# A chunked delta rule beside projection matmuls: row stores and half of T's loads on GpSimd's DMA queue, later loads of kq and of late decays, and the third group's masks behind the second substitution

## The chip, the cores and the metric

The kernel runs on one core of a Trainium2 chip. The metric is the device time of one execution in microseconds (us); less is better. The engines have short names in the profile: PE is TensorE (matmuls), DVE is VectorE, ACT is ScalarE, POOL is GpSimd, SP is SyncE, which here only issues DMAs. GpSimd issues DMAs too, on a queue of its own.

## The reference

One layer of a hybrid backbone: a SwiGLU FFN, then two mixers side by side (a 2-D neighbourhood attention and a bidirectional gated delta rule), merged by gates, then a second FFN; 512 latent and 256 context tokens of width 1024. The change lies in the delta rule, which the reference computes by chunks:

```python
def gated_delta_chunks(q, k, v, g, beta, s0, with_output):
    ...
    decay = jnp.exp(jnp.where(lower, g[..., :, None] - g[..., None, :], -jnp.inf))
    k_beta = k * beta[..., None]
    m = jnp.where(strict, jnp.einsum('...ik,...jk->...ij', k_beta, k) * decay, 0.0)
    rhs = jnp.concatenate([v * beta[..., None], k_beta * jnp.exp(g)[..., None]], axis=-1)
    uw = lax.linalg.triangular_solve(jnp.eye(GDN_CHUNK, dtype=m.dtype) + m, rhs,
                                     left_side=True, lower=True, unit_diagonal=True)
    ...
    def step(s, xc):
        v_new = xc[0] - jnp.einsum('...ck,...kv->...cv', xc[1], s)
        s_next = s * xc[3][..., None, None] + jnp.einsum('...ck,...cv->...kv', xc[2], v_new)
        ...
        return s_next, (jnp.einsum('...ck,...kv->...cv', xc[4], s)
                        + jnp.einsum('...cj,...jv->...cv', xc[5], v_new))
```

So for each chunk there is a gram matrix of the keys, weighted by decays and beta, a unit lower triangular matrix that has to be inverted, and a scan over the chunks that carries the state S.

## The kernel before, in words

The kernel uses chunks of 128 tokens: six steps s = 0 to 5 (two of context, four of latent tokens), two directions, and four heads in two pairs p = 0, 1. One instruction mostly works on the four matrices of a step and a pair. The steps are treated in three groups of two, called bi = 0, 1, 2 (first, second and third group). Each group passes through these stages:

- `gram` (from line 1114), four times in a group. A decay tile (`Dt`; for some steps a part of an `oacc` tile) is loaded from DRAM (`gcd`, line 1118), VectorE subtracts and masks it (line 1122), ScalarE takes the exponential, and VectorE multiplies it with the products of keys into `Bt` (line 1128), and with those of queries and keys into `At` (line 1134). The products come from TensorE for the steps 0 to 3 (`pq`), and the later steps read the stored ones back (`kq<-kqd`, lines 1096 to 1098), since the two directions meet the same pairs of chunks. `Bt` is stored to DRAM (`bd`).
- `base_inverse` (from line 1140), once in a group. It loads the 32-wide diagonal blocks of all the group's matrices out of `bd` (into `L` and `Ltr`, line 1152), sets L's diagonal to -1 (line 1155), and inverts them all at once by forward substitution on VectorE: 31 rows, each a product (line 1159) and a reduction (line 1160) whose length grows with the row. This is called the substitution here; there are three. The result `Xt` is stored to DRAM (`rd`, line 1163).
- `inverse` (from line 1173), twice in a group. It loads the inverted blocks back as T0 and T1 (`T<-rd`, line 1180, four loads), transposes them on VectorE (lines 1182, 1183), and puts the 128-wide inverse `Tt` together: TensorE `pi` products of 32 and then 64 columns, with copies `Y` and `T` by VectorE and ScalarE between them (lines 1202, 1218, 1229, 1237).
- `scan_step` (from line 1249), four times in a group. TensorE's `pc` products with the state, `r` (line 1260), the values `vn` (line 1269), the new state `S` (line 1284), and from step 2 on the output (`otmp` line 1291, `oacc` lines 1297, 1298).

Between these small steps TensorE does work that waits for nothing in the delta rule: matmuls of the input projection, called fills here (`pm` with `wh`, `wl`, lines 192 to 194; the weight half `wl` comes from VectorE, line 139). `turn` hands out so many fills after each small step.

A scheduler decides the order of the instructions on each engine from the order of the program, the sizes of the tile pools and a model of durations; `tc.issue_after(x)` puts an instruction behind x on its engine. Each engine then runs its own list strictly in order, and so do the DMA queues' issuers: a DMA that waits holds up all that stand behind it on SP. Tile pools matter for the change: `Dt` has two buffers, `kq` two, `r` two.

Of the kernel before, what the change touches and what calls it, by code (L numbers as in the profile page):

```python
# [13 lines left out]
ALU = mybir.AluOpType  # L14
AX = mybir.AxisListType.X
# [3 lines left out]
P = 128  # L19
# [39 lines left out]
def body(ctx, tc, I, out, dbg=None):  # L59
# [1020 lines left out]
    def products(p, s):  # L1080

        def one(n, a, o):
            if s == 1:
                return [kk01[p][:, m ^ 2] for m in range(4)]
            if s < 4:
                t = tl(pgq, [P, 4, P], "pq", 2)
                for m, (d, c, i) in enumerate(mats_of(s)):
                    mm(t[:, m, :], kT[2 * p + i][:, c], a[2 * p + i][:, c - o], start=True, stop=True)
                if s == 0:
                    kk01[p] = t  # L1090
                else:
                    u = tl(gb_, [P, 4, P], "kq", NKQ)
                    S.copy(u[:], t[:])
                    nc.sync.dma_start(kqd[n, s - 2, p], u[:].rearrange("p m c -> p (m c)"))
            else:
                t = tl(gb_, [P, 4, P], "kq", NKQ)
                for h in range(2):
                    nc.sync.dma_start(t[:, 2 * h:2 * h + 2].rearrange("p m c -> p (m c)"), kqd[n, 5 - s, p, :, 256 * (1 - h):256 * (2 - h)])
            return t
        yield one(0, kT, 0)  # L1100
        for _ in range(1 if s > 1 else 4 * s * p):
            turn("g", s // 2)
        if s >= 2:
            yield one(1, qT, 2)
            turn("g", s // 2)

    def decay_place(s, p):

        if s == 2 or s < 2 and p == 1:
            a = 2 * (s == 2)  # L1110
            return oaccs[p if s == 2 else s][:, a:a + 2].rearrange("p a b c -> p (a b) c")
        return tl(gb_, [P, 4, P], "Dt", 2)[:]

    def gram(p, s, bd, g):

        mats = mats_of(s)
        Dt = decay_place(s, p)
        nc.sync.dma_start(Dt[:], bass.AP(gcd.tensor, gcd.offset + (4 * s + 2 * p) * P, [[0, P], [24 * P, 2], [1, 2 * P]]))
        for m, (d, c, i) in enumerate(mats):
            msk = cst[:, (C_MF if d == 0 else C_MB):][:, 0:P]  # L1120
            with tc.issue_after(marks["At" if s > 3 else "Bt"]) if s > 1 else nullcontext():
                V.scalar_tensor_tensor(Dt[:, m], Dt[:, m], gcum[:, d, s, 2 * p + i:2 * p + i + 1], msk, op0=ALU.subtract, op1=ALU.add)
        S.activation(Dt[:], Dt[:], AF.Exp)
        Bt, At = tl(gq, [P, 4, P], "Bt", NBT), None
        for n, t in enumerate(products(p, s)):
            if n == 0:
                for m, (d, c, i) in enumerate(mats):
                    b = V.scalar_tensor_tensor(Bt[:, m], t[m] if s == 1 else t[:, m], beta[:, d, s, 2 * p + i:2 * p + i + 1], Dt[:, m], op0=ALU.mult, op1=ALU.mult)
                if s < 2:
                    marks["Bt"] = b.ins  # L1130
                nc.sync.dma_start(bass.AP(bd.tensor, bd.offset + g * MSTR, [[P, P], [4 * MSTR, 4], [1, P]]), Bt[:])
            else:
                At = tl(gq, [P, 4, P], "At", NAT)
                a = V.tensor_tensor(At[:], t[:], Dt[:], ALU.mult)
                if s < 4:
                    marks["At"] = a.ins
# [3 lines left out]
    def base_inverse(bd, rd):  # L1140
# [8 lines left out]
        st = 32 * P + 32  # L1149
        for q in range(4):  # L1150
            dst = tr[32 * q:32 * q + 32] if q < 2 else L[32 * q:32 * q + 32]
            nc.sync.dma_start(dst, bass.AP(bd.tensor, bd.offset + (q // 2) * 8 * MSTR, [[st, 32], [P, 32], [1, 32]]))
        S.copy(L[0:64].rearrange("p r c -> p c r"), tr[:])

        G.memset(L[:].rearrange("p r c -> p (r c)")[:, 0:1024:33], -1.0)
        for i in range(1, 32):
            c = (i + 1) // 2
            t = tl(gb_, [P, 16, 32], "bt")
            V.tensor_tensor(t[:, 0:c, 0:i + 1], L[:, i:i + 1, 0:i + 1].to_broadcast([P, c, i + 1]), Xt[:, 0:c, 0:i + 1], ALU.mult)
            V.tensor_reduce(Xt[:, 0:c, i], t[:, 0:c, 0:i + 1], AX, ALU.add, negate=True)  # L1160
            if i % 4 == 0:
                yield
        nc.sync.dma_start(bass.AP(rd.tensor, rd.offset, [[512, P], [1, 512]]), Xt[:].rearrange("p c k -> p (c k)"))
        yield


    T6s = [tl(gq, [P, 8, 64], f"T6{i}") for i in range(NT6)]
    Tts = [tl(gq, [P, 8, P], f"Tt{i}") for i in range(NTT)]
    for t in T6s + Tts:
# [3 lines left out]
    def inverse(bi, st, rd, Bts):  # L1173


        T0 = tl(gq, [P, 8, 32], "T0", 2)
        T1 = tl(gq, [P, 8, 32], "T1", 2)
        for dst, d in ((T1, 0), (T0, 1)):
            for q in range(2):
                nc.sync.dma_start(dst[q:P:2, 4 * d:4 * d + 4], bass.AP(rd.tensor, rd.offset + (2 * d + q) * 16384 + st * 2048, [[32, 64], [2 * 2048, 4], [1, 32]]))  # L1180
        fl = lambda t, m: t[:, m:m + 4].rearrange("p m c -> p (m c)")
        V.transpose(fl(T0, 0), fl(T1, 0))
        V.transpose(fl(T1, 4), fl(T0, 4))
        blk = [slice(32 * b, 32 * b + 32) for b in range(4)]

# [732 lines left out]
```

## Time and profile before

| | |
|---|---|
| median of 3 runs | 1499.26 us (1498.73 to 1499.43) |
| the profiled execution's own time | 1495.44 us |
| its span | 1493.7 us |
| TensorE's granted clock, mean | 0.993 |
| TensorE busy | 1434.0 us, 96% |
| VectorE busy | 1144.7 us, 77% |
| ScalarE busy | 661.9 us, 44% |
| GpSimd busy | 212.4 us, 14% |
| the delta rule's groups in the span | about 730 to 966 us |

How to read the rows. A row of the timeline gives the start and the length in us, the engine, the line, the operation with `out<-in`, the shape, the count, and in brackets the idle time before it and what ended it. A row of the waits gives engine, tile and line, what it waited for, then the us in total, the times and the longest. A row of the grouped view gives the count, the busy us, the mean ns of one, and the idle time before with its releaser. A row of the DMA issues gives the queue, the count, the KB of one and the median us from issue to landing.

### The profile page before, as it was taken

The numbers are of one execution on the slowest core, as the hardware profiler recorded it, in microseconds if no ns is written. First come the engines' busy times: TensorE is split into PE (matmuls) and PEld (weight loads), VectorE is DVE, ScalarE is ACT, GpSimd is POOL, SyncE is SP. The second block draws the span as 40 slices with busy tenths as digits, with TensorE's granted clock in tenths as the row PEclk, the third lists the DMA queues.
The fourth block names the chain that finished last, engine by engine and source line by source line (L and its number), as shares of the span: only waits on it lengthen the run. The fifth ranks groups of instructions, "written<-read, shape, count | busy, mean of one in ns | idle before, by whom it ended". The sixth has DMA issues, their size and how long they took to land.

```text
span 1493.7 us, 23926 instructions
## 1 busy us (share of the span) xinstructions
PE 1434.0 (96%) x9117; PEld 1258.3 (84%) x9117; DVE 1144.7 (77%) x1975; ACT 661.9 (44%) x1090; POOL 212.4 (14%) x262
## 2 busy tenths in 40 slices
PE   6999999999999999999998899999999999999997
PEld 4778989999998777888886778877778999998886
DVE  8787869999987565768787886666668799886627
ACT  5433524434333286545544434376526454444310
POOL 1000000000000121223301002243321022220001
PEclk9999999999999999999999999999999999999999
DMA  9676665454559554222577524274344143234732
GB/s 372 211 257 225 222 238 187 137 174 166 170 198 404 181 178 129 84 92 88 159 222 203 167 68 125 92 276 131 100 169 149 64 129 113 85 114 134 263 98 84
DMA packets 109236, 248.56 MB, mean 166 GB/s; under 512 B 29049, under 2 KB 44481, under 8 KB 109121
## 3 DMA queue, kind: packets, MB, share of 16 engines
q1 hardware_dynamic: 104480, 229.40, 46.6%
q0 software_dynamic: 3056, 12.33, 2.2%
q10 hardware_dynamic: 1586, 5.32, 0.9%
q8 instruction: 71, 1.16, 0.3%
q14 instruction: 43, 0.35, 0.1%
HBM read 215.50 MB, written 31.50 MB: 165 GB/s over the span
## 4 chain that ended last, share of the span: by engine, by line
PE 71%; DMA 10%; DVE 9%; ACT 4%; issue 3%; POOL 1%; SPq 1%; DVEq 0%; ACTq 0%; POOLq 0%
PE ps L211 15%; PE pm L192 5%; PE pm L193 5%; PE pm L194 5%; PE ps L533 4%; PE ps L535 4%; PE ps L534 4%; PE ps L1692 3%; PE ps L1694 3%; PE ps L1693 3%; PE ps L193 3%; PE ps L192 3%; PE ps L194 3%; PE pc L1049 3%; DMA wr<-in_up_dram 2%
## 5 line engine op out<-in xcount | busy, mean ns | idle before, releaser
L139 DVE TENSOR_TENSOR wl<-wr,wh 128x1024 fp32r<-128x1024 f32 (+1 forms) x184 | 226.0, 1233 | 112.9 <-ACT wh L137 111.3
L137 ACT CAST wh<-wr 128x1024 fp32r<-128x1024 f32 (+1 forms) x184 | 185.6, 1013 | 278.5 <-PE pm L193 72.7
L192 PE MATMUL pm<-uxh,wh 128*128 128x512 f32 x320 | 131.6, 411 | 0.0
L194 PE MATMUL pm<-uxh,wl 128*128 128x512 f32 x320 | 126.3, 395 | 0.8 <-DVE wl L139 0.8
L193 PE MATMUL pm<-uxl,wh 128*128 128x512 f32 x320 | 126.5, 395 | 0.0
L211 PE MATMUL ps<-wh,hx 128*128 128x512 f32 x352 | 96.1, 391 | 0.1
L211 PEld LDWEIGHTS ps<-wh,hx 128*128 128x128 f32 x352 | 65.9, 188 | 14.5 <-ACT wh L137 0.5
L280 DVE SCALAR_TENSOR_TENSOR adap<-wr,crow 128x1024 f32<-128x1024 f32 x61 | 74.3, 1218 | 2.4 <-DMA wr<-in_w_adaT_dram 1.7
L192 PE MATMUL ps<-uh,wh 128*128 128x256 f32 (+1 forms) x208 | 69.2, 334 | 3.8 <-ACT wh L137 3.8
L194 PEld LDWEIGHTS pm<-uxh,wl 128*128 128x128 f32 x320 | 60.6, 190 | 13.8 <-DVE wl L139 0.9
L192 PEld LDWEIGHTS pm<-uxh,wh 128*128 128x128 f32 x320 | 60.8, 190 | 11.1 <-ACT spill L796 0.2
L193 PEld LDWEIGHTS pm<-uxl,wh 128*128 128x128 f32 x320 | 60.9, 190 | 10.3
L114 POOL TENSOR_TENSOR rs<-ve,mhalf 128x1 f32<-128x1 f32 (+2 forms) x46 | 49.0, 1066 | 140.6 <-DVE ve L110 138.2
L193 PE MATMUL ps<-ul,wh 128*128 128x256 f32 (+1 forms) x208 | 67.9, 327 | 0.0
L194 PE MATMUL ps<-uh,wl 128*128 128x256 f32 (+1 forms) x208 | 67.0, 328 | 0.0
L193 PE MATMUL ps<-uxl,wh 128*128 128x256 f32 (+1 forms) x192 | 60.5, 318 | 2.2 <-DVE uxl L139 2.2
L192 PE MATMUL ps<-uxh,wh 128*128 128x256 f32 (+1 forms) x192 | 59.8, 318 | 1.6 <-ACT uxh L137 1.4
L194 PE MATMUL ps<-uxh,wl 128*128 128x256 f32 (+1 forms) x192 | 60.1, 316 | 0.0
L137 ACT CAST wh<-ra 128x1024 fp32r<-128x1024 f32 x31 | 32.6, 1052 | 59.7 <-PE ps L534 20.2
L533 PE MATMUL ps<-ur,wh 128*128 128x384 f32 x168 | 56.5, 336 | 0.0
L534 PE MATMUL ps<-ur,wh 128*128 128x384 f32 x168 | 56.4, 336 | 0.0
L533 PE MATMUL ps<-uh,wh 128*128 128x384 f32 x168 | 56.4, 336 | 0.0
(502 smaller groups left out, 4252.0 us busy)
## 6 DMA issues: line engine op xcount, KB each, us to landing
wr<-in_w_adaT_dram SPq DMA_DIRECT2D x64, 512.0 KB, 4.7
wr<-in_up_dram SPq DMA_DIRECT2D x56, 512.0 KB, 3.6
wr<-in_win_dram SPq DMA_DIRECT2D x52, 512.0 KB, 3.6
wr<-in_dn_dram SPq DMA_DIRECT2D x51, 512.0 KB, 4.1
ra<-in_up_dram SPq DMA_DIRECT2D x24, 512.0 KB, 4.3
rb<-in_up_dram SPq DMA_DIRECT2D x18, 512.0 KB, 4.0
ra<-in_w_adaT_dram SPq DMA_DIRECT2D x16, 512.0 KB, 5.0
wr<-in_w_o_dram SPq DMA_DIRECT2D x8, 512.0 KB, 4.4
```

What stands on the lines that cost most here:

```text
L114: G.tensor_tensor(rs[:], ve[:], mhalf[:, 0:n], ALU.pow)
L137: S.copy(hi, src)
L139: marks["lo"] = V.tensor_tensor(lo, src, hi.bitcast(F32), ALU.subtract).ins
L192: T.matmul(ps, a, uh[:, k, :], start=(k == 0), stop=False)
L193: T.matmul(ps, a, ul[:, k, :], start=False, stop=False)
L194: marks["mm"] = T.matmul(ps, b, uh[:, k, :], start=False, stop=(k == nk - 1)).ins
L211: T.matmul(banks[t][d][:, c0:c1], a[:, sl], b[:, d * 512 + c0:d * 512 + c1], start=first and j == 0, stop=last and j == 2)
L280: V.scalar_tensor_tensor(pr[:], raw[:], 1.0, crow, op0=ALU.mult, op1=ALU.mult, accum_out=col[:, c:c + 1])
L533: T.matmul(ps[:], a, mh, start=k == 0, stop=False)
L534: T.matmul(ps[:], a, ml, start=False, stop=False)
L535: T.matmul(ps[:], b, mh, start=False, stop=k == 3)
L1049: last[0] = T.matmul(*a, **k).ins
```

## The change

It has five parts.

1. Loads of the stored products for late steps (`kq<-kqd`) and of the decays of the steps 4 and 5 are issued behind the last load of `L` on SP.
2. The decay tile of step 3 is taken from the two `r` buffers instead of the two `Dt` buffers.
3. The masks of the third group are issued behind the last row of the second substitution (before: behind the last `At` of the second group). The stores of step 5's `Bt` are issued behind the last load of T on SP.
4. The store of the rows, `rd`, is issued by GpSimd, and T's loads are issued directly after it, those of T1 by SP and those of T0 by GpSimd. VectorE's first transpose of a pair is issued behind the last `Bt` of step 4's second pair.
5. L's diagonal is set by VectorE instead of GpSimd.

```diff
             else:
                 t = tl(gb_, [P, 4, P], "kq", NKQ)
                 for h in range(2):
-                    nc.sync.dma_start(t[:, 2 * h:2 * h + 2].rearrange("p m c -> p (m c)"), kqd[n, 5 - s, p, :, 256 * (1 - h):256 * (2 - h)])
+                    with tc.issue_after(marks["L"]):
+                        nc.sync.dma_start(t[:, 2 * h:2 * h + 2].rearrange("p m c -> p (m c)"), kqd[n, 5 - s, p, :, 256 * (1 - h):256 * (2 - h)])
...
+        if s == 3:
+            return tl(gq, [P, 4, P], "r", 2)[:]
         return tl(gb_, [P, 4, P], "Dt", 2)[:]
...
-        nc.sync.dma_start(Dt[:], bass.AP(gcd.tensor, gcd.offset + (4 * s + 2 * p) * P, [[0, P], [24 * P, 2], [1, 2 * P]]))
+        with tc.issue_after(marks["L"]) if s > 3 else nullcontext():
+            nc.sync.dma_start(Dt[:], bass.AP(gcd.tensor, gcd.offset + (4 * s + 2 * p) * P, [[0, P], [24 * P, 2], [1, 2 * P]]))
...
-            with tc.issue_after(marks["At" if s > 3 else "Bt"]) if s > 1 else nullcontext():
+            with tc.issue_after(marks["row" if s > 3 else "Bt"]) if s > 1 else nullcontext():
...
-                if s < 2:
+                if s < 2 or (s, p) == (4, 1):
                     marks["Bt"] = b.ins
-                nc.sync.dma_start(bass.AP(bd.tensor, bd.offset + g * MSTR, [[P, P], [4 * MSTR, 4], [1, P]]), Bt[:])
+                with tc.issue_after(marks["Tl"]) if s == 5 else nullcontext():
+                    nc.sync.dma_start(bass.AP(bd.tensor, bd.offset + g * MSTR, [[P, P], [4 * MSTR, 4], [1, P]]), Bt[:])
...
-        G.memset(L[:].rearrange("p r c -> p (r c)")[:, 0:1024:33], -1.0)
+        V.memset(L[:].rearrange("p r c -> p (r c)")[:, 0:1024:33], -1.0)
...
-        nc.sync.dma_start(bass.AP(rd.tensor, rd.offset, [[512, P], [1, 512]]), Xt[:].rearrange("p c k -> p (c k)"))
+        nc.gpsimd.dma_start(bass.AP(rd.tensor, rd.offset, [[512, P], [1, 512]]), Xt[:].rearrange("p c k -> p (c k)"))
+        for st in range(2):
+            T0 = tl(gq, [P, 8, 32], "T0", 2)
+            T1 = tl(gq, [P, 8, 32], "T1", 2)
+            for dst, d in ((T1, 0), (T0, 1)):
+                for q in range(2):
+                    t = (nc.gpsimd if d else nc.sync).dma_start(dst[q:P:2, 4 * d:4 * d + 4], bass.AP(rd.tensor, rd.offset + (2 * d + q) * 16384 + st * 2048, [[32, 64], [2 * 2048, 4], [1, 32]]))
+                    if not d:
+                        marks["Tl"] = t.ins
+            turned.append((T0, T1))
         yield
...
-        T0 = tl(gq, [P, 8, 32], "T0", 2)
-        T1 = tl(gq, [P, 8, 32], "T1", 2)
-        for dst, d in ((T1, 0), (T0, 1)):
-            for q in range(2):
-                nc.sync.dma_start(dst[q:P:2, 4 * d:4 * d + 4], bass.AP(rd.tensor, rd.offset + (2 * d + q) * 16384 + st * 2048, [[32, 64], [2 * 2048, 4], [1, 32]]))
+        T0, T1 = turned.pop(0)
         fl = lambda t, m: t[:, m:m + 4].rearrange("p m c -> p (m c)")
-        V.transpose(fl(T0, 0), fl(T1, 0))
+        with tc.issue_after(marks["Bt"]):
+            V.transpose(fl(T0, 0), fl(T1, 0))
```

How the order of the instructions changes is shown at three places. The numbers behind the names tell buffers and versions apart; lines of the changed kernel stand 4 to 12 higher.

VectorE at the start of the first substitution (`L_7133`), before: the weight cast `wl_7266` stands ahead of the first row.

```order
L139 TENSOR_TENSOR wl_7102<-wr_7099,wh_7101 128x1024
L1122 SCALAR_TENSOR_TENSOR Dt_7489<-Dt_7489,gcum_5208,cst_5205 128x128 x4
L139 TENSOR_TENSOR wl_7266<-wr_7263,wh_7265 128x1024
L1159 TENSOR_TENSOR bt_7147<-L_7133,Xt_7135 128x2
L1160 TENSOR_REDUCE Xt_7135<-bt_7147 128x1
L1159 TENSOR_TENSOR bt_7150<-L_7133,Xt_7135 128x3
```

And now, with the same cast named `wl_7278`:

```order
L1126 SCALAR_TENSOR_TENSOR r_7501<-r_7501,gcum_5208,cst_5205 128x128 x4
L139 TENSOR_TENSOR wl_7102<-wr_7099,wh_7101 128x1024
L1160 MEMSET L_7133 128x32
L1164 TENSOR_TENSOR bt_7147<-L_7133,Xt_7135 128x2
L1165 TENSOR_REDUCE Xt_7135<-bt_7147 128x1
L139 TENSOR_TENSOR wl_7278<-wr_7275,wh_7277 128x1024
L1164 TENSOR_TENSOR bt_7150<-L_7133,Xt_7135 128x3
```

The cast moved behind L's memset and the first row, and step 3's masks work on `r` buffers.

VectorE around the second substitution (`L_7789` before, `L_7795` now). Before, the masks of the third group's first two grams (the second is `Dt_8159`) stand ahead of its first row, and the other masks, with `Bt` and `At`, between its rows; here its start and a piece of its middle.

```order
L139 TENSOR_TENSOR wl_7572<-wr_7569,wh_7571 128x1024
L1122 SCALAR_TENSOR_TENSOR Dt_8159<-Dt_8159,gcum_5208,cst_5205 128x128 x4
L1159 TENSOR_TENSOR bt_7803<-L_7789,Xt_7791 128x2
...
L1218 TENSOR_SCALAR T_1275_6933<-pi_7901 32x4x32 x4
L1134 TENSOR_TENSOR At_8214<-kq_8211,Dt_8186 128x512
L1122 SCALAR_TENSOR_TENSOR Dt_8229<-Dt_8229,gcum_5208,cst_5205 128x128 x4
L1160 TENSOR_REDUCE Xt_7791<-bt_8033 128x11
L1159 TENSOR_TENSOR bt_8036<-L_7789,Xt_7791 128x12x24
```

Now, the last row of the second substitution and what follows it:

```order
L1165 TENSOR_REDUCE Xt_7797<-bt_8060 128x16
L1126 SCALAR_TENSOR_TENSOR Dt_8144<-Dt_8144,gcum_5208,cst_5205 128x128 x4
L1126 SCALAR_TENSOR_TENSOR Dt_8171<-Dt_8171,gcum_5208,cst_5205 128x128 x4
L1132 SCALAR_TENSOR_TENSOR Bt_8151<-kq_8152,beta_5207,Dt_8144 128x128 x4
L1139 TENSOR_TENSOR At_8163<-kq_8160,Dt_8144 128x512
...
L139 TENSOR_TENSOR wl_8231<-wr_8228,wh_8230 128x1024
L1139 TENSOR_TENSOR At_8196<-kq_8193,Dt_8171 128x512
L1126 SCALAR_TENSOR_TENSOR Dt_8198<-Dt_8198,gcum_5208,cst_5205 128x128 x4
L1272 SCALAR_TENSOR_TENSOR r_8279<-pc_8268,neg_5210,vtok_5217 128x128
L1272 SCALAR_TENSOR_TENSOR r_8279<-pc_8268,neg_5210,vtok_5218 128x128
```

All masks, `Bt` and `At` of the third group moved behind the second substitution, and the r of the next scan stands behind the third of its masks.

TensorE at the third group's first inverse (`pi_8870` before, `pi_8876` now). Before, it stands inside the last scan of the second group, with fills between its steps:

```order
L192 MATMUL pm_9053<-uxh_4690,wh_8979 128x512
L1049 MATMUL pi_8870<-T_1632_8854,Bt_8139 32x32 x4
L1049 MATMUL pi_8870<-T_1632_8854,Bt_8166 32x32 x4
...
L194 MATMUL pm_9053<-uxh_4690,wl_8980 128x512
L1049 MATMUL pc_9106<-vn_9076,At_7546 128x128 x4
L192 MATMUL pm_9053<-uxh_4690,wh_8979 128x512
```

And now:

```order
L1049 MATMUL pc_9112<-vn_9082,At_7558 128x128 x4
L192 MATMUL pm_9059<-uxh_4690,wh_8985 128x512
...
L194 MATMUL pm_9232<-uxh_4690,wl_9056 128x512
L1049 MATMUL pi_8876<-T_1601_8653,Bt_8151 32x32 x4
L1049 MATMUL pi_8876<-T_1601_8653,Bt_8178 32x32 x4
...
L1049 MATMUL pi_8895<-Y_1637_8893,T_1602_8654 32x32 x16
L1049 MATMUL pi_8896<-T_1602_8654,Y_1637_8893 32x32 x16
L1049 MATMUL pi_8937<-T_1275_6933,Bt_8151 64x64 x2
...
L1049 MATMUL pi_8948<-Tt_1276_6934,Y_1641_8946 64x64 x8
```

The first inverse of the third group moved behind the last scan of the second group (`pc_9106`, now `pc_9112`) and the fills after it, and its steps follow each other without fills. On VectorE the third substitution's last row stood ahead of the last two scans' outputs before, and stands behind both of them now.

More of the change, by code (lines that the diff above doesn't have):

```diff
@@ L1151, in base_inverse @@
             dst = tr[32 * q:32 * q + 32] if q < 2 else L[32 * q:32 * q + 32]
-            nc.sync.dma_start(dst, bass.AP(bd.tensor, bd.offset + (q // 2) * 8 * MSTR, [[st, 32], [P, 32], [1, 32]]))
+            marks["L"] = nc.sync.dma_start(dst, bass.AP(bd.tensor, bd.offset + (q // 2) * 8 * MSTR, [[st, 32], [P, 32], [1, 32]])).ins
         S.copy(L[0:64].rearrange("p r c -> p c r"), tr[:])
-        G.memset(L[:].rearrange("p r c -> p (r c)")[:, 0:1024:33], -1.0)
+        V.memset(L[:].rearrange("p r c -> p (r c)")[:, 0:1024:33], -1.0)
         for i in range(1, 32):
@@ L1159, in base_inverse @@
             V.tensor_tensor(t[:, 0:c, 0:i + 1], L[:, i:i + 1, 0:i + 1].to_broadcast([P, c, i + 1]), Xt[:, 0:c, 0:i + 1], ALU.mult)
-            V.tensor_reduce(Xt[:, 0:c, i], t[:, 0:c, 0:i + 1], AX, ALU.add, negate=True)
+            marks["row"] = V.tensor_reduce(Xt[:, 0:c, i], t[:, 0:c, 0:i + 1], AX, ALU.add, negate=True).ins
             if i % 4 == 0:
                 yield
-        nc.sync.dma_start(bass.AP(rd.tensor, rd.offset, [[512, P], [1, 512]]), Xt[:].rearrange("p c k -> p (c k)"))
+        nc.gpsimd.dma_start(bass.AP(rd.tensor, rd.offset, [[512, P], [1, 512]]), Xt[:].rearrange("p c k -> p (c k)"))
[8 more added lines that the diff above has]
+            turned.append((T0, T1))
         yield
+    turned = []
     T6s = [tl(gq, [P, 8, 64], f"T6{i}") for i in range(NT6)]
```

## The prediction

> **What bounds the kernel now.** The page comes first: TensorE is busy almost all the time.
>
> ```profile
> PE 1434.0 (96%) x9117; PEld 1258.3 (84%) x9117; DVE 1144.7 (77%) x1975; ACT 661.9 (44%) x1090; POOL 212.4 (14%) x262
> ```
>
> TensorE's matmuls are not touched by the change, so it can only be worth what TensorE waits, or what its clock loses by waiting. The second view is TensorE's waits in the delta rule, from 730 to 960 us:
>
> ```profile
> PE pi L1049 <- DVE Y L1229: 5.1, 3, 2.4
> PE pi L1049 <- DMA T<-rd: 4.3, 1, 4.3
> PE pc L1049 <- DVE bt L1159: 1.8, 1, 1.8
> PE pi L1049 <- DVE T L1218: 1.6, 2, 1.0
> ```
>
> These four rows are 12.8 us. The third view, busy time by stretch (time, PE, PEld, DVE, ACT, POOL, clock, DMA share, GB/s), adds what the clock takes:
>
> ```profile
> 800.00:806.00 6.00, 3.94 (x70) 2.76 (x70) 3.29 (x16) 2.18 (x5) 1.57 (x4) 0.72 0.70 176
> 850.00:870.00 20.00, 16.02 (x207) 13.29 (x206) 15.48 (x63) 8.28 (x22) 3.35 (x9) 1.00 0.36 97
> 870.00:875.00 5.00, 4.53 (x66) 3.71 (x65) 3.60 (x12) 1.01 (x3) 0.00 (x0) 0.66 0.02 3
> ```
>
> At 0.72 for 6 us and at 0.66 for 5 us, 1.7 us are lost each time. So some 16 us are at stake in the stage, and the rest of the program is outside the change but for the order of some loads of the attention.
>
> The fourth view is the timeline. VectorE runs three forward substitutions of 31 rows one after the other (first and last rows here, with the mask before the second):
>
> ```profile
> 755.99 0.16 DVE L1159 TENSOR_TENSOR bt<-L,Xt 128x2 f32<-128x2 f32 x1 [5.03 <-POOL L L1155]
> 790.12 0.69 DVE L1160 TENSOR_REDUCE Xt<-bt 128x16 f32<-128x512 f32 x1
> 795.86 1.14 DVE L1122 SCALAR_TENSOR_TENSOR Dt<-Dt,gcum,cst 128x128 f32<-128x128 f32 x4 [3.92 <-DMA Dt<-gcd]
> 797.11 0.16 DVE L1159 TENSOR_TENSOR bt<-L,Xt 128x2 f32<-128x2 f32 x1
> 848.48 0.68 DVE L1160 TENSOR_REDUCE Xt<-bt 128x16 f32<-128x512 f32 x1
> 852.66 0.16 DVE L1159 TENSOR_TENSOR bt<-L,Xt 128x2 f32<-128x2 f32 x1 [1.39 <-POOL L L1155]
> 900.62 0.68 DVE L1160 TENSOR_REDUCE Xt<-bt 128x16 f32<-128x512 f32 x1
> ```
>
> After each, a store (rd) and four small loads per pair (T) bring the result to TensorE's inverse. TensorE's waits near them, and two rows that the sums below go to, are:
>
> ```profile
> 802.00 0.92 PE L1049 MATMUL pi<-T,Bt 32*32 32x32 f32 x32 [4.33 <-DMA T<-rd]
> 828.45 0.68 PE L1049 MATMUL pi<-T,Bt 64*64 64x64 f32 x16 [0.99 <-DVE T L1218]
> 833.75 0.68 PE L1049 MATMUL pi<-Tt,Y 64*64 64x64 f32 x16 [2.37 <-DVE Y L1229]
> 851.33 1.05 PE L1049 MATMUL pc<-r,Tt 128*128 128x128 f32 x8
> 854.14 1.13 PE L1049 MATMUL pc<-vn,ktail 128*128 128x128 f32 x8 [1.75 <-DVE bt L1159]
> 867.21 0.68 PE L1049 MATMUL pi<-T,Bt 64*64 64x64 f32 x16 [0.62 <-DVE T L1218]
> 869.49 0.68 PE L1049 MATMUL pi<-Tt,Y 64*64 64x64 f32 x16 [1.60 <-DVE Y L1229]
> 871.03 2.08 PE L1049 MATMUL pc<-r,Tt 128*128 128x128 f32 x8 [0.47 <-ACT Tt L1237]
> 915.13 1.05 PE L1049 MATMUL pc<-vn,At 128*128 128x128 f32 x8
> 924.00 1.16 PE L1049 MATMUL pc<-r,Tt 128*128 128x128 f32 x8 [0.47 <-ACT Tt L1237]
> ```
>
> The third substitution costs TensorE next to nothing today: it ends at 901.3, before the last scans of the second group, which TensorE leaves at 915.13 + 1.05 = 916.2.
>
> **The change part by part. The row store and T's loads.** Before, after the first substitution:
>
> ```profile
> 792.49 2.92 SPq L1163 DMA_DIRECT2D rd<-Xt  x1
> 797.54 2.65 SPq L1180 DMA_DIRECT2D T<-rd  x4
> rd<-Xt SPq DMA_DIRECT2D x3, 256.0 KB, 4.5
> T<-rd SPq DMA_DIRECT2D x24, 32.0 KB, 2.3
> accd<-hx POOLq DMA_DIRECT2D x6, 512.0 KB, 3.0
> xr<-x1d POOLq DMA_DIRECT2D x4, 512.0 KB, 6.5
> ```
>
> The rows end at 790.8, SP takes up the store at 792.49 behind a decay load and two L loads, and the first four T loads go out one by one at 0.66 us. With the store on GpSimd's idle queue it starts at once (1.7 us earlier), and the four first loads go out two and two, which takes 1.3 us off the last of them; GpSimd's store of Xt and its loads do not occur before, so they lie between the rows of 3.0 and 6.5 us above; I take SP's own 4.5, which is nearest in size. The loads themselves are not cheaper: 2.3 us, and on GpSimd 3.0 at least for something larger. Against this, the weight cast (wl) ahead of the first row now stands behind the L memset in VectorE's order; TensorE waits for that cast some 2 us near 755 (an estimate out of the 5.03 of idle at 755.99, which the cast no longer precedes), and that comes off the 4.33 at 802. Of these 3.0 I take 2.5, since GpSimd's way to start a DMA isn't seen here, and T is there at 799.5 instead of 802.0: **-2.5**, and the clock's loss in the 800 to 806 row goes with the long stop: **-1.7**. Bounds: nothing (if the store lands after 6.5 us) to -6.0.
>
> The Trainium skill speaks against this part: "DMA: Bandwidth & Descriptors", section Issuing engines are not separate DMA queues, says that issuing from several engines saves only the sequencer's own time to start a DMA. The rows could be read otherwise, 3.0 us of landing for 512 KB on GpSimd against 4.5 for 256 KB on SP, which would be 1.5 more, -4.0; by the rule there is nothing to be had in the transfer, and I don't count it.
>
> **L's memset on VectorE.** 0.15 us move from GpSimd, where a hand-over stood between them (5.03 of idle at 755.99 is mostly L's load). I put it at nothing; it could be worth 0.3 us twice.
>
> **Third group's masks behind the second substitution, kq and late decays behind L.** By the grouped view of 745 to 930 us VectorE's work on that group is 16 of 24 masks, 16 Bt and 4 At, with their waits:
>
> ```profile
> L1122 DVE SCALAR_TENSOR_TENSOR Dt<-Dt,gcum,cst 128x128 f32<-128x128 f32 x24 | 6.8, 346 | 7.8 <-DMA Dt<-gcd 7.8
> L1128 DVE SCALAR_TENSOR_TENSOR Bt<-kq,beta,Dt 128x128 f32<-128x128 f32 x16 | 4.6, 343 | 0.0
> L1134 DVE TENSOR_TENSOR At<-kq,Dt 128x512 f32<-128x512 f32 x4 | 2.8, 692 | 1.9 <-DMA kq<-kqd 1.8
> ```
>
> 4.5 + 4.6 + 2.8 us of work and, inside the second substitution, 7.8 - 3.9 + 1.9 = 5.8 us or a little less of waiting leave it: 17 us. It also starts sooner: the mask ahead of its first row, with its wait of 3.92, was one of these, and its L goes out some 2 us earlier (an estimate), since the decay of the step before it, now in an r buffer, is loaded early and not between the stores. With L's way of 5.5 us from its issue to 797, that is 794.5 for 797.1. It ends near 829.5 instead of 849.2. The copies Y and T that TensorE waited for at 828 and 833 are no longer behind waits: **-3.4**. At TensorE's row of 851.33 the lead is 2.5 + 1.7 + 3.4 = 7.6, so it is ready at 843.7.
>
> All of it now stands behind, and it is loaded late. SP's queue holds the kq and decay loads behind T's loads, which wait for the store: store from 829.5, landing 834, four loads issued and landed 837, kq 839. The third decay, in one of two Dt buffers, goes out near 838.5.
>
> ```profile
> Dt<-gcd SPq DMA_DIRECT2D x4, 256.0 KB, 5.9
> kq<-kqd SPq DMA_DIRECT2D x16, 128.0 KB, 3.3
> L<-bd SPq DMA_DIRECT2D x6, 128.0 KB, 4.7
> bd<-Bt SPq DMA_DIRECT2D x10, 256.0 KB, 3.0
> ```
>
> It lands at 844.4; behind its masks on VectorE stands the r that TensorE's row of 851.33 reads. 844.4 + 1.1 (masks) + 1.1 (r) = 846.6 against 843.7: a new wait of **+2.9**. Bounds: +5 (6.5 us landing and a late kq) and 0 (landing in 3 us). Of the old 1.75 at 854 about 1.3 goes, since it came of VectorE waiting 1.39 for L; of the 0.6, 1.6 and 0.5 at 867 to 871, in the shadow of the third substitution's first rows, I let all go: **-1.3 - 2.7**. The lead into the last scans is 7.6 - 2.9 + 4.0 = 8.7, and TensorE would be through them at 916.2 - 8.7 = 907.5.
>
> **The third substitution.** The last Bt is written at about 855.6: the fourth decay's load can start only when an earlier Dt buffer is free (841.5, landing near 850), then come two r's, a cast, an S and four Bt. Store 3.0 + 0.9 to issue, L 4.7: L is there at 864.4, 12 us later than now. Its rows with the scans' work between them took 852.66 to 901.3, 48.6 us. VectorE was idle 4.5 of the 20 us from 850 to 870, most of it after 852.66; of that I take off 3.6, so 45 us, ending at 909.5 (up to 913 with nothing taken off). The order also puts its last row behind the last scan's output on VectorE, so it cannot end before 907.5 + 2. Here both meet, and from here nothing covers the way: store 4.5, two loads on each queue 0.6 + 2.3, transposes 0.6 make 917.5. TensorE has 12 fill matmuls and a scan product after the last scan, an estimate of 3.7 us, until 911.2. Stop: 6 us. Then the inverse's chain stands bare, with no fills between: the second half of such a chain, bare too, took from 867.21 to 871.03, 3.8 us; the first half has the same kinds of steps with one copy less, an estimate of 2.7. 917.5 + 6.5 = 924.0 for the row that was at 924.00. Of the lead nothing is left. **At 924 the sum is 0**, -1.5 to +4. The clock drops there as it did at 802 (+1.7) and no longer at 870, but that gain is spent in the same stop.
>
> By the Trainium skill, "TensorE: Matmul & The Clock Gate", section Part 1: The HAM clock gate, an idle window of about 3.4 us halves the clock. The row at 870 has 0.66 after stops of 1.6 us at most, which the rule does not give. By it the 1.7 us at 870 would not come back with those stops, which leaves the sum as it is, and takes 1.7 from the faster rival below.
>
> **Behind the stage.** The second attention block's ka and qa now stand ahead of the w_o loads, and the chain of waits had
>
> ```profile
> 1002.65 4.79 DMA qa<-qad
> 1010.66 0.43 PE L1472 MATMUL po<-pT,vw 128*64 128x128 f32 x2 [1.12 <-ACT pT L1463]
> ```
>
> which ends in a wait of TensorE of 1.12: **-1.1** at best. With +1.7 for the clock behind 924 at worst, these two nearly cancel; I take **-0.3**.
>
> Sum: -0.3 on the profiled execution's 1495.44 (span 1493.7 and 1.7 around it). That execution lies 3.8 below the median of 1499.26, so I set the difference on the median: **1499.0 us**. A measurement of this kernel tells about 0.2%, 3.0 us, from no change.
>
> **The rivals.**
> *Faster.* The third substitution is not as late as I make it. If the third decay lands in 3 us instead of 5.9 (the 16 DMA engines are at 0.36 in the row of 850 to 870, so there is room), VectorE gets on 3 us earlier, the r wait falls away and L comes at 861 or before; the bare stretch begins 3 us earlier, and the clock's loss at 870 (1.7) stays saved. -3 - 1.7 - 0.3: **1494.3**. For it: the small lateness of each load adds up over four steps; against it: 5.9 is the median of these very loads.
> *Slower.* The bare stretch at the third substitution is longer than the lead. It decides from an L at 866 or a store and load on GpSimd at the 6.5 us of xr instead of 4.5 and 2.3: two hops by 2 us, and the clock drop comes behind it (1.7): +2 +2 +1.7 - 0.3, **1504.7**. For it: nothing covers this stretch any more, so each us counts in full; against it: the queue of GpSimd has nothing else then.
> *It does not do what it says.* If GpSimd's queue gives nothing, and the second substitution is as long in its scans as now because TensorE paces it, all stays within 1 us: **1498.9**.
>
> **How the numbers follow.** Forecast 0.37, the empty case 0.06, faster 0.33, slower 0.24. 1494.3 and 1504.7 are the middles of their cases; taking in most of them, the range is 1493.5 to 1504.5, with the likeliest case's own at 1496.5 to 1501.5. Faster 0.33, same 0.43, slower 0.24.
>
> **What would show it.** Right: T's stop at 802 under 1 us with no clock drop, VectorE's second substitution ending before 832, its third starting after 862, a stop of TensorE of 4 to 8 us before the third inverse's first matmul at about 911, the row of 924.00 within 2 us of it. Wrong: a third substitution starting before 860 (then the faster rival), or that row later than 927 (the slower one).

## The result and the profile after

The changed kernel takes 1512.38 us (median of 5 runs, 1509.14 to 1516.73) against 1499.26 us: slower by 0.85%, ratio 1.0085, 95% interval 1.0062 to 1.0109. Its profiled execution took 1511.59 us, its span is 1509.8 us and the mean granted clock 0.983, where the kernel before had 1495.44, 1493.7 and 0.993.

The page's first line and TensorE's waits from 730 to 960 us of the changed kernel:

```profile
PE 1446.5 (96%) x9117; PEld 1268.5 (84%) x9117; DVE 1149.1 (76%) x1978; ACT 663.5 (44%) x1090; POOL 218.9 (14%) x274
```
```profile
PE pi L1049 <- DMA T<-rd: 5.9, 2, 4.9
PE pc L1049 <- DVE r L1272: 2.5, 4, 1.6
PE pi L1049 <- DVE Y L1214: 1.9, 2, 1.2
PE pc L1049 <- ACT Tt L1249: 1.9, 1, 1.9
PE pi L1049 <- DVE T L1194: 1.8, 1, 1.8
```

All of TensorE's waits in this stretch come to 19.1 us, where the kernel before has 16.1, only three more. But TensorE is busy 12.5 us longer with the same number of matmuls. The windows say where: the clock (the third column from the right) is half for a long while.

```profile
800.00:806.00 6.00, 3.83 (x72) 2.83 (x73) 3.73 (x17) 3.16 (x6) 1.94 (x7) 0.84 0.65 190
870.00:875.00 5.00, 3.37 (x39) 3.00 (x39) 3.93 (x16) 3.25 (x7) 0.00 (x0) 0.73 0.14 54
918.00:934.00 16.00, 6.32 (x168) 5.63 (x168) 4.13 (x15) 8.03 (x21) 8.73 (x15) 0.57 0.59 189
```

In the last row TensorE was busy 6.3 of 16 us, at 0.57 of its clock. The same stretch of the kernel before:

```profile
918.00:934.00 16.00, 14.30 (x287) 12.12 (x286) 8.70 (x23) 7.45 (x22) 1.41 (x2) 1.00 0.17 52
```

The timeline shows why. VectorE's first substitution runs as before, from 755.89 to 790.8. First and last rows of the second and the third:

```profile
795.43 0.16 DVE L1164 TENSOR_TENSOR bt<-L,Xt 128x2 f32<-128x2 f32 x1
832.86 0.68 DVE L1165 TENSOR_REDUCE Xt<-bt 128x16 f32<-128x512 f32 x1
870.91 0.16 DVE L1164 TENSOR_TENSOR bt<-L,Xt 128x2 f32<-128x2 f32 x1
915.82 0.69 DVE L1165 TENSOR_REDUCE Xt<-bt 128x16 f32<-128x512 f32 x1
```

The second substitution is 13.9 us shorter (38.1 for 52.0 us) and ends 15.6 us earlier; the third starts 18.3 us later and ends 15.2 us later, at 916.5. TensorE's stops, the last scan of the second group among them:

```profile
800.37 0.22 PE L1049 MATMUL pi<-T,Bt 32*32 32x32 f32 x2 [0.93 <-DMA T<-rd]
802.38 0.45 PE L1049 MATMUL pi<-T,Bt 32*32 32x32 f32 x30 [1.79 <-DVE T L1194]
850.15 1.26 PE L1049 MATMUL pc<-r,Tt 128*128 128x128 f32 x8 [1.62 <-DVE r L1272]
913.34 1.05 PE L1049 MATMUL pc<-vn,At 128*128 128x128 f32 x8
923.01 0.80 PE L1049 MATMUL pi<-T,Bt 32*32 32x32 f32 x32 [4.94 <-DMA T<-rd]
924.96 0.59 PE L1049 MATMUL pi<-Y,T 32*32 32x32 f32 x21 [1.15 <-DVE Y L1214]
927.14 1.12 PE L1049 MATMUL pi<-T,Bt 64*64 64x64 f32 x16 [1.10 <-DVE T L1230]
928.88 1.12 PE L1049 MATMUL pi<-Tt,Y 64*64 64x64 f32 x16 [0.61 <-DVE Y L1241]
932.44 2.08 PE L1049 MATMUL pc<-r,Tt 128*128 128x128 f32 x8 [1.87 <-ACT Tt L1249]
```

The last row is the one that was at 924.00 before. The stop of 4.94 us comes ahead of the third group's first inverse; its steps follow with nothing between them and at half clock (sixteen 64-wide products take 1.12 us where the same in the rows of before took 0.68).

Setting the same matmuls of the two traces side by side gives the difference along the program: +1.4 us at 730, when the stage begins (the clock dropped near 566 us in this execution), -1.2 at the scan row of 851.33 (the changed kernel is ahead, its row is at 850.15), -1.8 at the last scan's row of 915.13 (now 913.34), +8.4 at the row of 932.44, +10.3 at 970, +13.9 at 1050, +16.1 at the end. So the stage, from 730 to 970 us, costs 8.9, the first attention blocks, to 1050, 3.6, and 2.2 come later.

### The profile page after: what moved, and what is told of

Its sections match the earlier page's. It is cut to its first block, busy times and chain, and to the rows that moved or that the text cites. A ratio compares the mean times of both kernels' runs of the same rounds, so it can differ in the third digit from the quotient of the medians.

```text
span 1509.8 us, 23923 instructions
## 1 busy us (share of the span) xinstructions
PE 1446.5 (96%) x9117; PEld 1268.5 (84%) x9117; DVE 1149.1 (76%) x1978; ACT 663.5 (44%) x1090; POOL 218.9 (14%) x274
## 4 chain that ended last, share of the span: by engine, by line
PE 72%; DVE 10%; issue 7%; DMA 6%; ACT 3%; POOL 2%; SPq 1%; DVEq 0%; ACTq 0%; POOLq 0%
PE ps L211 17%; PE pm L192 5%; PE pm L194 5%; PE pm L193 5%; PE ps L534 5%; PE ps L535 5%; PE ps L533 5%; PE ps L1706 3%; PE ps L1705 3%; PE ps L1704 3%; PE ps L193 3%; PE ps L192 3%; PE ps L194 3%; DVE wl L139 2%; PE pc L1049 1%
```

## The experiments

Each kernel is compared with the kernel before that ran beside it on the same chip; the medians of that one were 1498.89, 1499.23, 1500.95 and 1499.87 us. What the stage and the attention cost in a trace is read as above, between 730, 970 and 1050 us, against the first trace of the kernel before.

**The masks back.** The changed kernel, with the masks and two waits as before:

```diff
-            with tc.issue_after(marks["row" if s > 3 else "Bt"]) if s > 1 else nullcontext():
+            with tc.issue_after(marks["At" if s > 3 else "Bt"]) if s > 1 else nullcontext():
...
-                with tc.issue_after(marks["Tl"]) if s == 5 else nullcontext():
+                with nullcontext():
...
-        with tc.issue_after(marks["Bt"]):
-            V.transpose(fl(T0, 0), fl(T1, 0))
+        V.transpose(fl(T0, 0), fl(T1, 0))
```

> The changed kernel with its third group's masks put back behind the second group's last At, and without the two waits that go with them (step 5's stores behind T's loads, T's transpose behind the Bt); the GpSimd queue, the loads behind L, the r buffers and the memset stay as changed. Theory: the 13 us come from the third substitution, which started at 870.9 us instead of 852.7 and ended at 916.5 instead of 901.3, so that TensorE stood 4.9 us before the third group's first inverse (923.0) and then ran a chain without fills at half clock. Then it starts near 853 to 856 again, that inverse has fills between its steps, the 4.9 us wait is gone, and the time is 1494 to 1500. Rival 1, GpSimd's queue costs the time (its stores land after 4 us and its loads are issued at 0.6 us each): still 1508 to 1514. Rival 2, the loads held behind L cost it: 1505 or more, with waits for kq or Dt on VectorE.

Measured: 1503.50 us, ratio 1.0017 (1.0003 to 1.0031). The stop is gone, and the third group's first inverse starts at 912.08 with no idle time named before it:

```profile
858.64 0.16 DVE L1164 TENSOR_TENSOR bt<-L,Xt 128x2 f32<-128x2 f32 x1
```
```profile
912.08 0.45 PE L1049 MATMUL pi<-T,Bt 32*32 32x32 f32 x32
916.39 1.26 PE L1049 MATMUL pc<-r,Tt 128*128 128x128 f32 x8 [1.15 <-DVE r L1271]
```

So most of the loss went with the masks and the two waits. The third substitution starts 2.6 us later than expected and the time is 3.5 us above the range, so something else is left: the stage costs 1.2 us here, and the attention still 3.2.

**The queues back.** `nc.gpsimd` of the row store and of T0's loads is `nc.sync` again, all else as changed.

> The changed kernel with the row stores and all of T's loads on SP's queue; all else as changed. Theory (the late third substitution): 1510 to 1516, the third substitution starts at 869 to 876, the stop before the third group's first inverse stays, 4 to 8 us. Rival 1 (GpSimd's queue costs the time): 1497 to 1502.

Measured: 1506.60 us, ratio 1.0050 (1.0034 to 1.0065); the third substitution starts at 872.63, the stop is 4.76 us. The theory's mechanism stands; the time lies between the two expectations, which the kernels under "Which piece of the queues" take up.

**The queue alone.** The kernel before with the store and half of T's loads on GpSimd and L's memset on VectorE; the masks, loads and buffers of before.

```diff
-        nc.sync.dma_start(bass.AP(rd.tensor, rd.offset, [[512, P], [1, 512]]), Xt[:].rearrange("p c k -> p (c k)"))
+        nc.gpsimd.dma_start(bass.AP(rd.tensor, rd.offset, [[512, P], [1, 512]]), Xt[:].rearrange("p c k -> p (c k)"))
...
+                    t = (nc.gpsimd if d else nc.sync).dma_start(dst[q:P:2, 4 * d:4 * d + 4], bass.AP(rd.tensor, rd.offset + (2 * d + q) * 16384 + st * 2048, [[32, 64], [2 * 2048, 4], [1, 32]]))
...
+        V.memset(L[:].rearrange("p r c -> p (r c)")[:, 0:1024:33], -1.0)
```

> The kernel before with the row stores and half of T's loads on GpSimd's queue, T's loads issued right behind the store, and L's memset on VectorE; masks, loads of kq and decays and buffers as before. Theory: this part is a small gain, the wait for T at 802 goes from 4.3 us to 1 to 3 and nothing else gets longer: 1495 to 1498. Rival 1: 1508 or more.

Measured: 1499.86 us, ratio 0.9996 (0.9981 to 1.0011): no difference, where a small gain was expected. The wait for T is 3.0 us instead of 4.3, and nothing of it arrives at the end: in the trace the stage costs 0.1 us and the attention 4.2.

**The loads free.** Both `issue_after(marks["L"])` taken out, the masks late as changed.

> The changed kernel with its loads of kq and late decays not held behind L's loads; masks still behind the second substitution. Theory: of the lateness of the third substitution a part is made by loads that stand behind T's loads on SP (VectorE waited 3.65 us for kq at 845.3 and 1.45 at 855.3); with them free it starts 2 to 5 us earlier, near 866 to 869, and the time falls by as much, to 1506 to 1511. Rival 2 (the loads held behind L cost nearly all): 1500 or less. If the place of these loads on SP's queue does not change by this, no difference: 1510 to 1514.

Measured: 1508.87 us, ratio 1.0062 (1.0040 to 1.0084), in the theory's range, but not by its way: the third substitution starts at 871.17. The kq loads stand behind T's loads on SP here too (T's at 836.5, kq's at 840.5), so this edit did not test what it was meant to.

**The changed kernel and the kernel before again.** No edit; for second traces.

> The changed kernel again, unaltered, to have its time beside the others and a second trace. Theory (the loss is in the program's order): the third substitution starts within 1.5 us of 870.9 and the stop before the third group's first inverse is 4 to 6 us again; time 1507 to 1514. If the loss is chance clock drops of the one trace: under 1503.

Measured: 1513.76 us, ratio 1.0093 (1.0071 to 1.0114); the third substitution at 867.01, 3.9 us earlier than in the first trace where 1.5 was the bound (1.8 of it are there at the first substitution already), the stop 4.86 us. Its stage costs 5.3 us and the attention 3.4.

> The kernel before again, for a second trace: how much of the 3.5 us between 975 and 1010 us and of the 1.4 us near 566 us by which the changed kernel's trace is longer comes in the kernel before too. Chance (the clock's drops): this trace is longer than the first by 1 to 4 us in these places. Order of the attention's loads: it is not, to 0.5 us.

Measured: 1498.34 us. The clock drop near 566 us is there (+1.7 against the first trace), so that one is chance. The attention from 970 to 1050 is as long as in the first trace, to 0.1 us, which speaks against chance for the longer stretch of the changed kernel.

**The masks alone.** The kernel before with the masks behind the last row:

```diff
-            with tc.issue_after(marks["At" if s > 3 else "Bt"]) if s > 1 else nullcontext():
+            with tc.issue_after(marks["row" if s > 3 else "Bt"]) if s > 1 else nullcontext():
...
-            V.tensor_reduce(Xt[:, 0:c, i], t[:, 0:c, 0:i + 1], AX, ALU.add, negate=True)
+            marks["row"] = V.tensor_reduce(Xt[:, 0:c, i], t[:, 0:c, 0:i + 1], AX, ALU.add, negate=True).ins
```

> The kernel before with one part of the change: the third group's masks behind the last row of the second substitution. Theory (the late third substitution): the third substitution starts 10 us or more later than 852.7, TensorE stops 4 to 8 us before the third group's first inverse, time 1504 to 1512. Rival (the move costs only together with the loads held back or GpSimd's queue): within 3 us of the kernel before.

Measured: 1508.34 us, ratio 1.0062 (1.0046 to 1.0079). This one edit makes two thirds to four fifths of the loss (0.62% against 0.78 to 0.93% in the three timings of the changed kernel); in its trace the stage costs 6.7 us and the attention 2.6:

```profile
868.48 0.15 DVE L1159 TENSOR_TENSOR bt<-L,Xt 128x2 f32<-128x2 f32 x1
```
```profile
922.84 0.65 PE L1049 MATMUL pi<-T,Bt 32*32 32x32 f32 x32 [2.98 <-DMA T<-rd]
```

The stop is smaller than expected (2.98 us). The bare chain is there too, but it is shorter than the changed kernel's: 7.0 us from this row to the next one shown, for 9.4, though both ran at 0.50 of the clock.

```profile
929.79 2.07 PE L1049 MATMUL pc<-r,Tt 128*128 128x128 f32 x8 [0.28 <-ACT Tt L1237]
```

**All of T on GpSimd's queue.** `(nc.gpsimd if d else nc.sync)` is `nc.gpsimd`, and step 5's stores don't wait.

> The changed kernel with all of T's loads on GpSimd's queue, so that SP's queue does not wait for the row store any more, and without the wait of step 5's stores behind them. In the changed kernel the kq loads stood on SP behind T's loads, which waited for the store to land at 838; they went out at 841.8 and VectorE waited 3.65 us for them. Theory: they go out near 837, the third substitution starts 3 to 6 us earlier, at 865 to 868, and the time falls by 2 to 5 us against the changed kernel in the same call. If the wait on SP is not on the way: no difference to 1 us.

Measured: 1506.25 us, ratio 1.0048 (1.0033 to 1.0063), 7.5 us below the changed kernel that ran beside it. SP's queue now has the kq loads at 836.08, where the changed kernel had them at 841.75:

```profile
835.64 0.39 SPq L1136 DMA_DIRECT2D bd<-Bt  x1
836.08 2.12 SPq L1099 DMA_DIRECT2D kq<-kqd  x4
```
```profile
837.97 2.61 SPq L1174 DMA_DIRECT2D T<-rd  x4
840.68 0.55 SPq L802 DMA_DIRECT2D gad<-spill  x1
841.32 0.38 SPq L1136 DMA_DIRECT2D bd<-Bt  x1
841.75 2.04 SPq L1099 DMA_DIRECT2D kq<-kqd  x4
```

(the second fence is the changed kernel). The third substitution starts at 864.07, and the time falls by more than expected. In the traces the stage costs 2.8 us, for 5.3 to 8.9 in the three traces of the changed kernel. Two things changed at once here, T's loads and the wait of step 5's stores; what each is worth was not separated. And not everything got faster: from the end of the third substitution to TensorE's first product with T it took 12.3 us (907.55 to 919.88) for 6.5, since T's loads took 4.1 to 5.6 us to land for 2.1 to 3.0, with loads of the attention going out on SP from 906.86 on.

**Which piece of the queues.** The changed kernel a third time, with both queues back, with only the store back on SP, and with only T's loads back on SP.

> The changed kernel once more, beside the three that follow, since the kernel with both queues back (0.50% slower than before) and the changed kernel (0.85 and 0.93%) were timed in different calls. 1509 to 1514.

> Stores and loads of T all on SP's queue again, in one call with the changed kernel. If GpSimd's queue costs something in the changed order (rival 1 in a small form): 3 to 8 us below the changed kernel of this call. If the two calls differed by chance: within 2 us of it.

> The changed kernel with the row store on SP, half of T's loads still on GpSimd. If the store on GpSimd is what costs: as the kernel with both back; if T0's loads are: as the changed kernel.

> The changed kernel with all of T's loads on SP, the row store still on GpSimd. If T0's loads on GpSimd are what costs: as the kernel with both back; if the store is: as the changed kernel. The third group's T is then issued on SP at 0.65 us each, 2.6 us for four, so the stop before the third group's first inverse may grow by 1 us.

Measured, in this order: 1512.07 us, 1.0078 (1.0060 to 1.0095); 1510.47, 1.0059 (1.0037 to 1.0080); 1512.11, 1.0075 (1.0050 to 1.0099); 1511.41, 1.0071 (1.0053 to 1.0088). All four intervals overlap. Both queues back are 1.6 us below the changed kernel beside them, within the 2 us that were expected of chance. That GpSimd's queue itself costs something in the changed order is not shown: in the two traces with both queues back the stage costs 8.2 and 7.0 us, no less than in the changed kernel's (5.3 to 8.9), and the attention 2.4 and -0.4 for 2.9 to 3.6. In the attention these two have TensorE's order of the kernel before, which the next experiment is about.

**The attention's stop.** TensorE in the first attention block, before:

```profile
978.83 0.66 PE L1429 MATMUL pt<-ident,vst 128*128 128x128 f32 x4 [2.60 <-ACT pT L1463]
979.41 0.39 PE L1446 MATMUL sc<-kch,qa 64*128 64x256 f32 x2
979.73 0.78 PE L192 MATMUL pm<-uxh,wh 128*128 128x512 f32 x1
980.31 1.06 PE L1429 MATMUL pt<-ident,vst 128*128 128x128 f32 x4
981.01 0.78 PE L193 MATMUL pm<-uxl,wh 128*128 128x512 f32 x1
981.59 0.63 PE L194 MATMUL pm<-uxh,wl 128*128 128x512 f32 x1
982.15 1.12 PE L1472 MATMUL po<-pT,vw 128*64 128x128 f32 x8
```

and in the changed kernel:

```profile
989.76 0.66 PE L1441 MATMUL pt<-ident,vst 128*128 128x128 f32 x4 [2.42 <-ACT pT L1475]
990.77 0.66 PE L1441 MATMUL pt<-ident,vst 128*128 128x128 f32 x4 [0.35 <-ACT pT L1475]
993.23 1.12 PE L1484 MATMUL po<-pT,vw 128*64 128x128 f32 x8 [1.80 <-DVE vw L1442]
```

The last three fills and two score products, which stood in this stop, were put ahead of it by the scheduler; the expectations call this the flip. The edit holds the last six fills there, three more than the kernel before has; it was made on the changed kernel, on the kernel before and on the kernel with the queue alone:

```diff
+        if (m, b) == (0, 3):
+            marks["sc"] = scores
...
-            for _ in fills:
-                pass
+            while done[0] < len(FILLS) * FS - 1:
+                next(fills)
+            with tc.issue_after(marks["sc"]):
+                for _ in fills:
+                    pass
```

> The changed kernel with the last six fill matmuls held behind the fourth score product of the first attention block. In the kernel before three fills and two score products stood in TensorE's stop there (978.8 to 982.2), in the changed kernel none do, and the stretch from 970 to 1050 is 2.7 to 3.5 us longer in two traces. Theory (a second, smaller part of the loss is this order): 2 to 3.5 us below the changed kernel's +0.8 to +0.9%, so +0.6 to +0.7%, 1508 to 1510 where before is 1499. If the stretch is longer for another reason: no difference.

Measured: 1505.64 us, ratio 1.0040 (1.0024 to 1.0055), below the changed kernel's 1.0078 to 1.0093 by 6 to 8 us, more than expected. The stretch from 970 to 1050 is 2.1 us shorter than before's where the changed kernel's was 3.6 longer, and its clock is full:

```profile
984.51 0.50 PE L192 MATMUL pm<-uxh,wh 128*128 128x512 f32 x1
986.30 1.15 PE L1441 MATMUL pt<-ident,vst 128*128 128x128 f32 x8 [1.29 <-ACT pT L1475]
```

> The kernel before with the same six fills held there. It has three of them there already: -1 to +0.5 us against before.

Measured: 1498.41 us, ratio 0.9994 (0.9981 to 1.0008): no difference.

> The kernel before with only the GpSimd queue part and the memset (equal to before when run alone), and the fills held. Its trace had the longer attention stretch too (+2.8 us). Theory: 1.5 to 3 us faster than before, 1496 to 1497.5. If the flip costs nothing in the median: equal to before to 1 us.

Measured: 1497.16 us, ratio 0.9980 (0.9964 to 0.9996), faster than the kernel before by 2.7 us and the only kernel here that is. It was expected that the flip had eaten what the queue gave. The traces don't show that: the stage costs 0.1 us without the fills held and 0.0 with them, so the queue gave nothing there that arrived; the difference lies in the attention, 4.2 and -1.4 us. The intervals of the two kernels with the queue part overlap.

**The change without its losing part.** The changed kernel with the masks, the loads of kq and of late decays as before, without the two waits, and with the six fills held.

> The changed kernel without the part that loses: masks of the third group, loads of kq and late decays as before, with the GpSimd queue, step 3's decay in r buffers, the memset on VectorE and the fills held. VectorE has the first two grams' masks ahead of the second substitution and all Dt buffers free for the third group, so the waits of 3.06 and 3.92 us for decays should go, and the third group's first inverse stands far ahead of the last scans. Theory: second substitution shorter by 3 us, third starting at 850 or before, time 2 to 5 us below before, 1494 to 1497. Rival: the decays' loads collide earlier and the third starts no sooner: within 2 us of before.

Measured: 1500.48 us, ratio 1.0012 (0.9996 to 1.0027): no difference, the rival. The third substitution starts at 854.35, no sooner than before, and the wait for T is 6.0 us.

## Why the prediction was wrong

The forecast was no change; its slower rival named the place and the mechanism, the bare stretch at the third substitution, and priced it too low. Of its signs, the late third substitution and a stop of 4 to 8 us came (4.94, but from 918 on and not from 911); the second substitution's end before 832, the row of 924.00 within 2 us and a full clock at 802 did not. By its own steps:

- **The store and T's loads** (-2.5 and -1.7). Side by side, the changed kernel's matmuls are 1.8 us late at 795 and 0.2 at 805: 1.6 us instead of 4.2, the clock's part in it, whose loss in the 800 to 806 row only went from 1.7 to 1.0 us. The store did land 2.9 us earlier (794.6 for 797.5), but SP then still issued kq loads, T's first loads took 4.4 to 5.2 us to land for 2.3 to 3.2 before, and VectorE's transposes of T started at 802.0 only:

```profile
802.01 0.31 DVE L1194 STREAM_TRANSPOSE T<-T 128x128 f32<-128x128 f32 x1 [2.26 <-DMA T<-rd]
```

  So TensorE's stop under 1 us (0.93) has a second one behind it (1.79). The 2 us that TensorE was said to wait for the weight cast near 755 were read off VectorE's idle time; TensorE's own wait for it there is 0.75 us before and 1.36 now. As a part of its own, with L's memset, this part gave nothing measurable (0.9996). The rule of the Trainium skill in "DMA: Bandwidth & Descriptors", Issuing engines are not separate DMA queues, by which nothing is to be had in the transfer, held for T in the changed kernel's trace: 2.4 us on GpSimd beside 2.5 on SP in the median. With all of T on GpSimd's queue the median was 5.3 us, beside other loads on SP, and no run separates the two. The store took 3.5 us on GpSimd, and 2.8 to 4.5 in the traces with it on SP.

```profile
rd<-Xt POOLq DMA_DIRECT2D x3, 256.0 KB, 3.5
T<-rd POOLq DMA_DIRECT2D x12, 32.0 KB, 2.4
T<-rd SPq DMA_DIRECT2D x12, 32.0 KB, 2.5
```

- **The second substitution** was to end at 829.5 and ended at 833.5: it started 0.9 later, and was 38.1 us long, not 35. TensorE's lead was smaller than forecast too: the row of 851.33 was to come at 846.6 and came at 850.15, and TensorE left the last scan at 914.4, not at 907.5. That did not decide the row of 924, since TensorE then stood waiting for T.
- **The failed step: "The last Bt is written at about 855.6 ... L is there at 864.4".** The last Bt was written at 861.8 and L was there at 870.7. 4 us are the second substitution's end; 2 are the kq loads, which landed at 845.2 instead of 839. (The prediction's own terms from 855.6 add up to 864.2.) The prediction did put the kq loads behind T's loads on SP, which wait for the row store of the same substitution that the masks wait for, but it gave 5 us from the first of T's loads to kq's landing (834 to 839). It took 7.3 (838.0 to 845.2): 3.8 until SP had issued the four loads of T and two other DMAs, and 3.5 to land, where its own row of kq had 3.3. The rows:

```profile
845.33 0.61 DVE L1132 SCALAR_TENSOR_TENSOR Bt<-kq,beta,Dt 128x128 f32<-128x128 f32 x2 [3.65 <-DMA kq<-kqd]
855.30 0.69 DVE L1139 TENSOR_TENSOR At<-kq,Dt 128x512 f32<-128x512 f32 x1 [1.45 <-DMA kq<-kqd]
870.79 0.09 DVE L1160 MEMSET L<- 128x32 f32 x1 [2.91 <-ACT L L1158]
```

  The kernel with all of T on GpSimd, and with step 5's stores let go, fits this: kq went out 5.4 us behind the second substitution's end for 8.2, and the time fell by 7.5 us. The decays, which the prediction feared instead, did not hold VectorE up in this trace.

  That the late third substitution is what the stage pays for shows over all traces. Counted from the first row of the first substitution, the third starts 96.1 to 100.9 us later in the seven traces with early masks, where the stage costs 0.0 to 1.2 us; in the eleven with late masks it starts 107.5 to 116.2 us later, and the stage costs from 2.8 us (at 107.5) to 9.6 (at 116.2).
- **The third substitution's length** was right: 45.6 us for 45; VectorE was busy for 40.8 of them. So its end was 916.5 for 909.5, and the way from there to T 6.5 us for 8.0.
- **The bare chain** was priced at full clock, 6.5 us, with the clock's drop only in the 1.7 us put behind 924 "at worst". It took 9.4 us (923.0 to 932.4). The clock was at 0.50 from 920.5 to 937 us, but that is the smaller part of it: with the masks alone the chain ran at 0.50 too and took 7.0. What came on top is waits inside the chain, above all for ScalarE, whose last copy into `Tt` stood behind its copy of the attention's `va`:

```profile
930.28 1.33 ACT L1396 COPY vst<-va 128x256 f32<-128x256 f32 x4 [0.30 <-DMA va<-vad]
931.62 0.77 ACT L1249 ACTIVATE Tt<-pi 64x256 f32<-64x256 f32 x2
```

  TensorE waited 1.87 us for it, where it waited 0.28 with the masks alone; there ScalarE was through with `va` at 923.3. Another 1.9 us were lost behind the row of 932.44. This is the term that was mis-sized; the rival's 1504.7 had 1.7 for the clock and nothing for ScalarE. The substitution's end 7.0 us late, the way to T 1.5 shorter and the chain 2.9 longer make the 8.4 us by which the row of 924.00 came late.
- **The attention** was put at -1.1 to 0 because two loads stood earlier. It is +2.9 to +3.6 in the three traces of the changed kernel. The order of the matmuls there was not compared; only that of the loads was. In the ten traces with the flip this stretch costs 2.6 to 5.2 us, at a clock of 0.94 to 0.96; in the eight where fills stand in the stop it costs -2.1 to +2.4, at 0.96 to 1.00.

So of 13 us the lateness of the third substitution makes 5 to 9, in the stage, and the order in the attention some 3, by the traces of the changed kernel; holding six fills there gained 2 more than the kernel before's order in its trace. That order came with ten of the edited kernels' traces, with the late masks alone and with the queue alone, but not with both queues back. 2 to 4 us behind 1050 us in the changed kernel's traces, in part by a slower pace near 1300, stay open.

What the forecast had right is the structure, in its slower rival's words: "nothing covers this stretch any more, so each us counts in full". It forecast that gain and loss cancel, out of two estimates of more than 8 us each; 6 us more in a chain of loads and stores were enough to upset that.

## What to carry to other kernels

Work that is moved out of a busy stretch to make it shorter starts a new chain, and the chain's length has to be summed over every queue that it passes, with what waits at the head of each queue: here T's loads, waiting for a store, in front of kq's. Where the last cover over a chain of small dependent products goes, price it at the throttled clock, and look at what the other engines of the chain have to do by then. And after any edit compare the order of the whole program where a scheduler makes it, since a stop two stages on can lose the work that filled it.

## What the runs showed of the hardware

- The clock's drop is partly chance: near 566 us, with the same three stops (1.4, 0.2 and 1.3 us), the first trace of the kernel before has none and its second trace has one, 1.7 us apart. The times of the unaltered kernel before spread from 1494.75 to 1506.08.
- The drop behind the long stop is not: from 918 to 934 us the clock is 0.53 to 0.68 in all eleven traces with late masks and 1.00 in the seven with early ones. In the changed kernel it lasted through the stop's end and the whole chain, 6.3 us of work in 16 us.
- In the attention, from 970 to 1050 us, the clock was 1.00 in the changed kernel with six fills held in the stop, against 0.96 without:

```profile
970.00:1050.00 80.00, 75.94 (x636) 58.76 (x635) 57.13 (x83) 55.96 (x127) 30.55 (x37) 1.00 0.62 209
```
```profile
970.00:1050.00 80.00, 73.14 (x582) 56.63 (x581) 53.16 (x77) 52.10 (x117) 30.41 (x38) 0.96 0.58 191
```

  The first row is the changed kernel with the fills held, the second the changed kernel. The same six fills left the clock at 0.98 on the kernel before and on the one with the queue alone, and both queues back gave 0.96 in one trace and 1.00 in the other, so chance has a part in this too.
- A DMA that waits holds up those behind it on its issuer: SP's kq loads went out at 841.75 behind T's loads, and at 836.08 where T's loads were on GpSimd's queue.
